# A hybrid encoder layer on one core: other order of PSUM banks in the out projection's second half, later sums for the first MLP tiles, other order of products in the last MLP tile

## The chip, the core and the metric

The kernel runs on one core of a Trainium2 chip. The metric is the device time of one execution in microseconds (us). Five engines share the work, each with an instruction stream of its own: PE (TensorE, matrix products), DVE (VectorE), ACT (ScalarE), POOL (GpSimd) and SP (SyncE, which here only issues DMAs). A semaphore ties an instruction to whatever it has to wait for. The results of PE stand in PSUM banks until DVE or ACT reads them.

## The reference

One encoder layer on 1024 tokens of width 1024, all in fp32: a norm, one projection, two kinds of attention side by side, an out projection with a residual, a gated MLP of inner width 2816 with a short convolution over the tokens, and a last norm.

```python
hn = rmsnorm(h, norm_mix[l])
proj = jnp.einsum('bsd,de->bse', hn, w_in[l])
...
o_a = window_gqa_sink(qa, ka, va, sink[l])
o_b = neighbourhood_attention(...)
mix = jnp.concatenate([rmsnorm(o_a, norm_a[l]), rmsnorm(o_b, norm_b[l])], axis=-1)
h = h + jnp.einsum('bse,ed->bsd', mix, w_out[l])
hn = rmsnorm(h, norm_ffn[l])
# conv_gated_mlp:
g = jnp.einsum('bsd,df->bsf', hn, w_gate)
u = jnp.einsum('bsd,df->bsf', hn, w_up)
g = conv over the tokens, width 3, one filter per channel, + conv_b
h = h + jnp.einsum('bsf,fd->bsd', jax.nn.silu(g) * u, w_down)
return rmsnorm(h, norm_final)
```

## The kernel before, in words

**Layout.** Everything is kept transposed: 128 channels on the partitions, the 1024 tokens along the free axis, in two halves of 512. A PSUM bank holds one 128x512 result. There are four names (tags) of banks with two banks each: `pj`, `o`, `s` and `pt`. Who asks for a bank of a name gets the older of the two, and has to wait until its last reader is done.

**Precision.** Each fp32 factor is split in a high and a low part (`whi`, `wlo` for weights; `hg`, `xd` for operands): ACT makes the high part by a copy (L786), DVE the low part by a subtraction (L787). A block of 128x128 weights is then three matmuls on 512 columns: whi by the high operand (L797, in the attention part L113), whi by the low operand (L798, L114), wlo by the high operand (L799, L115). A product of four blocks is 12 matmuls. So the first matmul of a product waits for `whi`, and the third for `wlo`.

**Who sets the order.** PE runs in the order in which the program is written (`manual_schedule` for PE). On DVE, ACT, POOL and SP a scheduler orders the instructions, starting from the program's order. Buffers come from pools with a fixed number for each tag: 16 `xg`, 14 `op` and 8 `mix` (128x1024 each), 6 `tt` (128x512), 3 `raw` weights, 9 `wh` and 9 `wl`. A load or a result waits until the buffer that it takes over has been read for the last time.

**Out projection.** Its first half (`OutA`, result added by DVE in L490) runs as filler in the attention. The second half is the loop from L857 over the token halves h (2) and the output tiles d (8): a product of 4 blocks in a bank whose name changes from product to product (L861), then `settle_out` (L816) for it: DVE adds the bank to h1, ACT writes h1 to DRAM and squares it for the next norm.

**MLP, gate and up.** Gate and up, the two halves of the tokens and the two halves of the inner dimension make a 2x2 by 2x2 block product, which is done with 7 products in place of 8 (Winograd's form). For a tile of 128 of the 2816 channels (there are 22) `Gated` has these seven methods, each a product of 12 matmuls and what reads its bank:
- `p1`: x = w11 by B11; ACT copies x to c (L937)
- `p5`: y = s1 by t1; DVE adds to c (L947)
- `p6`: z = s2 by t2; DVE makes the second half of gs (L953)
- `p2`: x += w12 by B21; ACT copies x to gs (L942)
- `p3`: y += s4 by B22; DVE adds to gs (L957)
- `conv`: ACT (L963), DVE twice (L964, L965), ACT with Silu (L966), on 128x1024
- `p7`: z += s3 by t3; DVE adds to c (L970)
- `p4`: z += w22 by t4; DVE adds to c (L975) and multiplies c by the conv's result (L976); `keep` writes c to DRAM (a DMA issued by ACT)

A product that adds to a bank has to wait until the reader of the bank's first state is done: `p2` for L937, `p7` for L953, `p3` for L947, `p4` for L970.

The weights of a tile come from `Weights`, one step each: load (SP), w11, w12, s1 (a DVE sum, L903), s2 (L907), s4 (L911), s3 (L916), 22, all but the load with a split. The steps for the next tile are called between the products of the present one (`more`, `w_next.step`).

The tiles are taken in pairs, k and k+11. The first four tiles (`units`, `HEAD` = 4) go product by product through all four; then the main loop (L1126) takes the tiles 4 to 21 one by one, in the order p1, p5, p4 of the tile before (`pend`), p6, p2, p3, conv, p7. In the last tile (21) there are no weights left to prepare, and the order is p1, p2, p5, p4 of tile 20, p6, p7, p3; the first loads for the down projection stand between (`prepare`: weights, `x_load`: operands, both issued by SP).

**Sums.** The down projection has the same seven products, with w_down and the MLP's result as factors. What it needs of a pair are differences: `sums` (L994 ff) makes t2, t3 and t4 for a pair from the two c tiles (three DVE subtractions of 128x512, L835), and `keep` writes them to DRAM (two DMA issues on ACT, one for t2 and t3, one for t4). In the head it is called after `p4` of units 1 and 3; in the main loop after `p4` of a pair's second tile, that is, in every other tile from tile 6 on.

**MLP, down.** 84 groups (7 products, 4 column blocks, 3 parts of K) of up to 12 matmuls. Weights are loaded 6 groups ahead and split 4 groups ahead (`prepare(i + 6, i + 4)`); operands are loaded (`x_load`, L1104, into an `xg` or an `op` buffer) and split (`x_split`, L1110 on ACT, L1111 on DVE) during the product before. `leave` and `finish` add, norm and write the output.

Of the kernel before, what the change touches and what calls it, by code (L numbers as in the profile page):

```python
# [20 lines left out]
KT = D // 128  # L21
# [30 lines left out]
def hybrid_layer(tc, xT, w_in, w_out, w_gate, w_up, w_down, small, sink, rpb, consts, rope, out):  # L52
    nc = tc.nc
    with ExitStack() as ctx:
# [19 lines left out]
        def bank(name, tag):  # L74
            return psum.tile([128, HALF], F32, name=name, tag=tag)
# [41 lines left out]
        def product(ps, ws, xs, h):  # L117

            for i, (w, x) in enumerate(zip(ws, xs, strict=True)):
                block(ps, w, x, h, i == 0, i == len(ws) - 1)  # L120
                yield
# [23 lines left out]
        def inverse_narrow(sqs, dim, tag):  # L145

            ps = bank("ss", tag)
            for c in range(4):
                for i, sq in enumerate(sqs):
                    nc.tensor.matmul(ps[:, c:c + 1], sq[:, c * 128:(c + 1) * 128], ones[:, 0:1], start=c == 0 and i == 0,  # L150
                                     stop=i == len(sqs) - 1, skip_group_check=True)
            v = cpool.tile([128, 4], F32, name="v4", tag="v4", bufs=4)
            nc.scalar.activation(v, ps[:, 0:4], AF.Sqrt, bias=eps, scale=float(D) / dim)
            nc.vector.reciprocal(v, v)
            return v

        def widen(v, tag):

            wide = bank("sw", tag)
            for c in range(4):  # L160
                nc.tensor.matmul(wide[:, c * 128:(c + 1) * 128], v[:, c:c + 1].to_broadcast([128, 128]), ident, start=True, stop=True)
            return wide
# [496 lines left out]
        units = []  # L659
# [38 lines left out]
        sums = {}  # L698
# [10 lines left out]
        pend = None  # L709
        run_q(q_until(1, 4 + AHEAD))  # L710
        fill(FILL1)
        for u in range(len(flat)):
# [14 lines left out]
            for what, e in events:  # L727
                if what == "t":
                    nxt = e()
                elif what == "v":  # L730
                    if pend is not None:
                        pend()
                    pend = nxt
# [14 lines left out]
        def load_wo(d, pools):  # L748
            raw = pools.tile([128, 4, 128], F32, name="raw", tag="raw", bufs=2 if pools is wpool else 3, padded_shape=[128, 4 if pools is wpool else 8, 128])
            nc.sync.dma_start(raw, w_out[d, :, 4:8, :])  # L750
            t = big("wo", "op", F32R)[:, :].rearrange("p (s j c) -> p s j c", s=2, c=128)
            nc.scalar.activation(t[:, 0], raw, AF.Copy)
            nc.vector.tensor_tensor(t[:, 1], raw, f32(t[:, 0]), op=ALU.subtract)
            return [(t[:, 0, j, :], t[:, 1, j, :]) for j in range(4)]
# [46 lines left out]
        def operand(src, tag):  # L801

            t = big("hg", tag, F32R)
            nc.scalar.activation(t[:, 0:HALF], src, AF.Copy)
            nc.vector.tensor_tensor(t[:, HALF:S], src, f32(t[:, 0:HALF]), op=ALU.subtract)
            return t[:, 0:HALF], t[:, HALF:S]
# [7 lines left out]
        def settle_out():  # L814
            d, h, ps = late.pop(0)
            nc.vector.tensor_tensor(at(d, h), ps, at(d, h), op=ALU.add)  # L816
            nc.scalar.dma_start(spilled[d][:, tsl(h)], at(d, h))
            s2 = half("s2")
            nc.scalar.activation(s2, at(d, h), AF.Square)
            if total[h] is not None:  # L820
                nc.vector.tensor_tensor(s2, s2, total[h], op=ALU.add)
            total[h] = s2

        def normed(h, wide, ds):
            for d in ds:
                nc.vector.scalar_tensor_tensor(at(d, h), at(d, h), col(C_NFFN + d), wide, op0=ALU.mult, op1=ALU.mult)

        def pure(f):
            raw = load_raw(w_gate[f], KT)
            W[f, "11"], W[f, "12"] = split_w(raw[:, 0:4], 4), split_w(raw[:, 4:8], 4)  # L830
# [8 lines left out]
        def head_weights(i, name):  # L839
            f, t = FO[i], wsum[i]  # L840
            if name == "s1":
                u = load_raw(w_up[f], KT)
                nc.vector.tensor_tensor(t, u[:, 0:4], u[:, 4:8], op=ALU.add)
            elif name == "s2":
                g = load_raw(w_gate[f, :, 0:4], 4)
                sub(t, t, g)
            elif name == "s4":
                g = load_raw(w_gate[f, :, 4:8], 4)
                sub(t, g, t)
            elif name == "s3":  # L850
                g, u = load_raw(w_gate[f, :, 0:4], 4), load_raw(w_up[f, :, 0:4], 4)
                sub(t, g, u)
            else:
                t = load_raw(w_up[f, :, 4:8], 4)
            W[f, name] = split_w(t, 4)

        for h in range(2):  # L857
            for d in range(KT):
                if h == 0 and d + 2 < KT:
                    wo.append(load_wo(d + 2, fpool))  # L860
                ps = bank("pj", ("pj", "o", "s")[(h * KT + d) % 3])  # L861
                for _ in product(ps, wo[d], mg[4:8], h):
                    pass
                late.append((d, h, ps))
                if h == 1 and d == 1:
                    v = inverse_narrow([total[0]], D, "pt")
                settle_out()
                if h == 0 and d in (3, 4):
                    pure((0, FT // 2)[d - 3])
                if h == 0 and d >= 5 or h == 1 and d == 0:  # L870
                    head_weights((d - 5) % KT, "s1")
                if h == 1 and d == 2:
                    wide = widen(v, "pt")
                    normed(0, wide, K1)
                    B[1, 1] = [operand(at(k, 0), "xg") for k in K1]
                if h == 1 and d == 4:
                    normed(0, wide, K2)
                    B[2, 1] = [operand(at(k, 0), "xg") for k in K2]
# [116 lines left out]
        def sums(unit):  # L995
            k = unit.f % FH
            a, b = first_of.pop(k), unit.c
            t = big("t23", "mix")
            sub(t[:, 0:HALF], b[:, HALF:S], a[:, HALF:S])
            sub(t[:, HALF:S], t[:, 0:HALF], a[:, 0:HALF])  # L1000
            keep(t, ("t2", k), ("t3", k))
            t4 = half("t4")
            sub(t4, b[:, 0:HALF], t[:, 0:HALF])
            keep(t4, ("t4", k))

        units = [Gated(f, ("o", "o", "pj", "pj")[i], ("s", "s", "pt", "pt")[i]) for i, f in enumerate(FO[:HEAD])]
# [44 lines left out]
        w_next = Weights(FO[HEAD])  # L1051
        for i, u in enumerate(units):
            u.p4()
            if i % 2:
                sums(u)
            w_next.step(3)
            if i < 2:
                units[i + 2].conv()
# [42 lines left out]
        def x_load(p, k):  # L1101
            t = big("xd", "xg" if counts[0] % (2 * FH) < 16 else "op", F32R)
            counts[0] += 1
            nc.sync.dma_start(f32(t[:, HALF:S]), X[PRODUCTS[p][1], k])  # L1104
            xraw[p, k] = t
# [10 lines left out]
        def prepare(loads, weights):  # L1116

            while loaded[0] < min(loads, len(order)):
                down_raw(*order[loaded[0]])
                loaded[0] += 1  # L1120
            while made[0] < min(weights, len(order)):
                down_weights(*order[made[0]])
                made[0] += 1

        pend = None
        for i, f in enumerate(FO[HEAD:]):  # L1126
            u = Gated(f)
            w_next.step(9)
            last_one = i + 1 == FT - HEAD
            w_next = None if last_one else Weights(FO[HEAD + i + 1])  # L1130
            more = lambda n=1: w_next.step(n) if w_next else None
            more()
            u.p1()
            if last_one:
                u.p2()
                prepare(2, 0)
            more()
            u.p5()
            if pend:
                pend.p4()  # L1140
                if pend.f >= FH:
                    sums(pend)
            more()
            u.p6()
            if last_one:
                for k in range(6):
                    x_load(0, k)
            more()
            if not last_one:
                u.p2()  # L1150
            more()
            if last_one:
                u.p7()
            u.p3()
            u.conv()
            if last_one:
                prepare(3, 1)
            more()
            if not last_one:
                u.p7()  # L1160
            else:
                for k in range(4):
                    x_split(0, k)
                prepare(4, 2)
                for k in range(6, FH):
                    x_load(0, k)
            more()
            pend = u
# [58 lines left out]
        for i, (p, j, c) in enumerate(order):  # L1227
# [6 lines left out]
            ps = banks[p, j]  # L1234
# [118 lines left out]
```

## Time and profile before

The span goes from the first to the last instruction of the profiled execution.

| what | value |
|---|---|
| time, median of 3 runs | 1135.11 us (1134.78 to 1135.58) |
| time of the profiled execution | 1135.27 us |
| its span | 1133.5 us |
| mean granted TensorE clock | 0.983 |
| busy: PE, PE's weight loads, DVE | 1087.3, 904.3, 853.2 us |
| busy: ACT, POOL | 549.9, 105.9 us |

The stages behind the attention, from the trace (busy time of PE, DVE and ACT in each, and the share of time in which the DMA engines moved data):

| stage | from, to (us) | length | PE | DVE | ACT | DMA |
|---|---|---|---|---|---|---|
| out projection, second half | 426.9 to 472.3 | 45.4 | 45.4 | 38.2 | 22.0 | 62% |
| first four MLP tiles | 472.3 to 545.0 | 72.7 | 72.5 | 66.2 | 34.1 | 28% |
| p4 of the head's last, tiles 4 to 20 | 545.0 to 880.5 | 335.5 | 330.5 | 270.0 | 131.2 | 30% |
| last tile, 21 | 880.5 to 906.5 | 26.0 | 22.4 | 21.0 | 15.7 | 73% |
| down projection and end | 906.5 to 1133.5 | 227.0 | 215.1 | 158.2 | 97.5 | 67% |

How to read what follows. A list of waits gives, for each group of instructions, the engine, the operation with its line, then `<-` and what released it, then the sum of the waits in us, their number and the longest. A table of stretches gives, for each, the length, then the busy time (and the number of instructions) of PE, PE's weight loads, DVE, ACT and POOL, then the granted clock of PE (1.00 is full), the busy share of the DMA engines and GB/s. A timeline has the start in us, the duration, the engine, the line, the operation, its output and inputs with their shapes.

### The profile page before, as it was taken

What the parts mean: (1) busy time and instruction counts of PE and PEld (TensorE: products, weight loads), DVE (VectorE), ACT (ScalarE), POOL (GpSimd) and SP (SyncE); (2) the same over time, 40 slices, a digit from 0 to 9 for tenths busy, and PEclk for the clock granted to TensorE, in tenths of its full rate; (3) what the DMA queues carried; (4) which work ended last, traced back from release to release, by engine and by line L of the source; (5) the groups of instructions that cost most, each with busy time, mean ns of one, the idle gap of its engine ahead of it and who ended that gap; (6) DMA issues with size and microseconds to landing.
All of it is one profiled execution on the core that took longest, in us unless ns stands there. A gap on an engine that the chain in (4) does not pass through costs nothing.

```text
span 1133.5 us, 14918 instructions
## 1 busy us (share of the span) xinstructions
PE 1087.3 (96%) x5124; PEld 904.3 (80%) x5124; DVE 853.2 (75%) x1549; ACT 549.9 (49%) x1033; POOL 105.9 (9%) x186
## 2 busy tenths in 40 slices
PE   8969999999999989999899999999999899999995
PEld 6857888888878878888688888888888688888884
DVE  5556888766689667899988778877877868886843
ACT  6335777656667534444443344334343645543531
POOL 0302333232223100000000000000000000000001
PEclk8989999999999999999899999999999999999997
DMA  7252120333215217303432223222322698865723
GB/s 262 61 126 79 52 57 29 80 93 88 74 36 150 94 47 256 134 29 109 181 128 103 102 93 121 103 102 93 121 103 93 222 322 280 280 226 169 258 83 148
DMA packets 67708, 147.03 MB, mean 130 GB/s; under 512 B 8112, under 2 KB 16816, under 8 KB 67632
## 3 DMA queue, kind: packets, MB, share of 16 engines
q1 hardware_dynamic: 57552, 121.04, 33.4%
q10 hardware_dynamic: 10080, 25.04, 5.9%
q8 instruction: 40, 0.66, 0.2%
q14 instruction: 36, 0.29, 0.1%
HBM read 103.58 MB, written 28.57 MB: 117 GB/s over the span
## 4 chain that ended last, share of the span: by engine, by line
PE 87%; DVE 6%; DMA 2%; ACT 2%; issue 1%; SPq 0%; POOLq 0%; ACTq 0%; DVEq 0%
PE pj L113 7%; PE pj L114 7%; PE pj L115 7%; PE dn L797 6%; PE dn L799 6%; PE dn L798 6%; PE z L797 4%; PE z L798 4%; PE z L799 4%; PE s L273 3%; PE x L797 3%; PE x L798 3%; PE x L799 3%; PE y L799 3%; PE y L798 3%; PE y L797 3%
## 5 line engine op out<-in xcount | busy, mean ns | idle before, releaser
L786 ACT ACTIVATE whi<-ws 128x512 fp32r<-128x512 f32 (+1 forms) x100 | 60.1, 623 | 126.2 <-DVE ws L903 86.0
L797 PE MATMUL dn<-xd,whi 128*128 128x512 f32 x308 | 120.0, 390 | 0.0
L799 PE MATMUL dn<-xd,wlo 128*128 128x512 f32 x308 | 119.8, 389 | 0.0
L798 PE MATMUL dn<-xd,whi 128*128 128x512 f32 x308 | 119.8, 389 | 0.0
L797 PE MATMUL z<-hg,whi 128*128 128x512 f32 x264 | 103.2, 391 | 2.2 <-DVE gs L953 2.2
L113 PE MATMUL pj<-xgh,whi 128*128 128x512 f32 x248 | 103.7, 418 | 0.0
L799 PE MATMUL z<-hg,wlo 128*128 128x512 f32 x264 | 103.2, 391 | 0.2 <-DVE wlo L787 0.2
L798 PE MATMUL z<-hg,whi 128*128 128x512 f32 x264 | 103.0, 390 | 0.0
L299 ACT ACTIVATE p<-p,nm 128x385 f32<-128x385 f32 (+3 forms) x128 | 75.1, 587 | 55.5 <-DVE nm L295 51.5
L115 PE MATMUL pj<-xgh,wlo 128*128 128x512 f32 x248 | 97.8, 394 | 0.0
L114 PE MATMUL pj<-xgl,whi 128*128 128x512 f32 x248 | 97.5, 393 | 0.0
L303 POOL TENSOR_SCALAR p<-p,sm 128x384 f32<-128x384 f32 (+1 forms) x128 | 73.2, 584 | 237.1 <-DVE sm L301 217.9
L787 DVE TENSOR_TENSOR wlo<-raw,whi 128x512 fp32r<-128x512 f32 (+1 forms) x102 | 66.7, 672 | 24.2 <-ACT whi L786 24.2
L786 ACT ACTIVATE whi<-raw 128x512 fp32r<-128x512 f32 (+1 forms) x102 | 61.0, 612 | 45.3 <-DMA raw<-in_w_down_dram 11.0
L787 DVE TENSOR_TENSOR wlo<-ws,whi 128x512 fp32r<-128x512 f32 (+1 forms) x100 | 67.0, 683 | 20.6 <-ACT whi L786 20.4
L309 DVE TENSOR_TENSOR pl<-pt,ph 128x384 fp32r<-128x384 f32 (+2 forms) x108 | 63.2, 588 | 23.2 <-ACT ph L308 22.1
L308 ACT ACTIVATE ph<-pt 128x384 fp32r<-128x384 f32 (+2 forms) x108 | 55.2, 513 | 38.4 <-PE pt L408 30.9
L1209 POOL TENSOR_TENSOR y<-y,wide 128x512 f32<-128x512 f32 x4 | 5.1, 1280 | 734.1 <-ACT y L1208 734.1
L1110 ACT ACTIVATE xd<-xd 128x512 fp32r<-128x512 f32 x77 | 47.5, 627 | 53.5 <-DMA xd<-x 51.7
L797 PE MATMUL y<-hg,whi 128*128 128x512 f32 x176 | 69.3, 394 | 2.9 <-ACT whi L786 2.9
L799 PE MATMUL y<-hg,wlo 128*128 128x512 f32 x176 | 69.6, 395 | 2.2 <-DVE wlo L787 2.2
L797 PE MATMUL x<-hg,whi 128*128 128x512 f32 x176 | 68.8, 391 | 1.4 <-ACT c L937 1.4
(199 smaller groups left out, 2660.7 us busy)
## 6 DMA issues: line engine op xcount, KB each, us to landing
xd<-x SPq DMA_DIRECT2D x77, 256.0 KB, 4.9
raw<-in_w_down_dram SPq DMA_DIRECT2D x72, 256.0 KB, 3.5
raw<-in_w_gate_dram SPq DMA_DIRECT2D x22, 512.0 KB, 3.5
raw<-in_w_up_dram SPq DMA_DIRECT2D x22, 512.0 KB, 3.8
x<-c ACTq DMA_DIRECT2D x22, 512.0 KB, 2.8
raw<-in_w_in_dram SPq DMA_DIRECT2D x32, 256.0 KB, 3.2
raw<-in_w_down_dram SPq DMA_DIRECT2D x36, 192.0 KB, 3.8
x<-t ACTq DMA_DIRECT2D x11, 512.0 KB, 5.8
```

What stands on the lines that cost most here:

```text
L113: nc.tensor.matmul(ps, w[0], x[0][:, tsl(h)], start=first, stop=False)
L114: nc.tensor.matmul(ps, w[0], x[1][:, tsl(h)], start=False, stop=False)
L115: nc.tensor.matmul(ps, w[1], x[0][:, tsl(h)], start=False, stop=last)
L299: nc.scalar.activation(p[:, j, 0:e], p[:, j, 0:e], AF.Exp, bias=nm, scale=-1.0, accum_out=sm[:, j:j + 1])
L303: nc.gpsimd.tensor_scalar(p[:, i, 0:m], p[:, i, 0:m], sm[:, i:i + 1], 1.0, op0=ALU.mult, op1=ALU.mult)
L308: nc.scalar.activation(ph[:, 0:n], ps[:, 0:n], AF.Copy)
L309: nc.vector.tensor_tensor(pl[:, 0:n], ps[:, 0:n], f32(ph[:, 0:n]), op=ALU.subtract)
L786: nc.scalar.activation(hi, src, AF.Copy)
L787: nc.vector.tensor_tensor(lo, src, f32(hi[:, :, :]), op=ALU.subtract)
L797: nc.tensor.matmul(ps, w[0], x[0], start=first and i == 0, stop=False, skip_group_check=True)
L798: nc.tensor.matmul(ps, w[0], x[1], start=False, stop=False, skip_group_check=True)
L799: nc.tensor.matmul(ps, w[1], x[0], start=False, stop=last and i == len(ws) - 1, skip_group_check=True)
```

## The change

Three edits, all in the program's order. None adds or removes a computation.

1. The banks of the out projection's second half go in the order `o`, `s`, `pj` in place of `pj`, `o`, `s`.
2. `sums` of the head's units 1 and 3 is no longer called behind their `p4`, but in the main loop behind `p6` of tile 4 (for unit 1) and of tile 5 (for unit 3).
3. In the last tile p2 goes where the other tiles have it (behind p6), so that the order is p1, p5, p4 of tile 20, p6, p2, p7, p3. The first two loads of down weights stand behind p5 and p4 in place of p2, and of the six operand loads, four stay behind p6 and two go behind p2.

```diff
@@ -858,7 +858,7 @@
-                ps = bank("pj", ("pj", "o", "s")[(h * KT + d) % 3])
+                ps = bank("pj", ("o", "s", "pj")[(h * KT + d) % 3])
@@ -1051,8 +1051,6 @@
         for i, u in enumerate(units):
             u.p4()
-            if i % 2:
-                sums(u)
             w_next.step(3)
@@ -1122,7 +1120,7 @@
-        pend = None
+        pend, owed = None, [units[1], units[3]]
         for i, f in enumerate(FO[HEAD:]):
@@ -1131,25 +1129,27 @@
             u.p1()
-            if last_one:
-                u.p2()
-                prepare(2, 0)
             more()
             u.p5()
             if pend:
                 pend.p4()
                 if pend.f >= FH:
                     sums(pend)
+            if last_one:
+                prepare(2, 0)
             more()
             u.p6()
+            if owed:
+                sums(owed.pop(0))
             if last_one:
-                for k in range(6):
+                for k in range(4):
                     x_load(0, k)
             more()
-            if not last_one:
-                u.p2()
+            u.p2()
             more()
             if last_one:
+                for k in range(4, 6):
+                    x_load(0, k)
                 u.p7()
             u.p3()
             u.conv()
```

Line numbers in what follows are those of the kernel before; from the second edit on the changed kernel's are two lower in the functions of the down projection.

## The prediction

> **What bounds the kernel now.** First the page: its chain of work that ended last is PE for 87%, and PE is busy 96% of the span. Time can come only from stretches in which PE stands or runs slowly, so the second view is the list of what PE waited for, over the whole span. All of it is 30 us; five of its lines lie behind the attention:
> ```profile
> PE 87%; DVE 6%; DMA 2%; ACT 2%; issue 1%; SPq 0%; POOLq 0%; ACTq 0%; DVEq 0%
> ```
> ```profile
> PE pj L113 <- DVE h L490: 3.5, 2, 3.2
> PE y L797 <- ACT whi L786: 2.9, 1, 2.9
> PE y L799 <- DVE wlo L787: 2.2, 1, 2.2
> PE z L797 <- DVE gs L953: 2.2, 1, 2.2
> PE x L797 <- ACT c L937: 1.4, 1, 1.4
> ```
> The two y waits stand at 553.9 to 559.9, in the first tile of the main loop (tile 4): its weights s1 are not split. The last two are in the last tile (tile 21), at 883.2 and 895.9. The third view is a table of stretches (PE, PEld, DVE, ACT, POOL busy, then the granted clock):
> ```profile
> 418.90:422.30 3.40, 1.93 (x9) 1.26 (x7) 3.40 (x7) 1.90 (x3) 0.00 (x0) 1.00 0.00 0
> 422.30:425.70 3.40, 1.66 (x7) 1.39 (x8) 2.89 (x5) 0.63 (x1) 0.00 (x0) 1.00 0.00 0
> 555.45:558.85 3.40, 0.73 (x2) 0.30 (x2) 3.40 (x5) 0.63 (x1) 0.00 (x0) 1.00 0.58 231
> 558.86:565.68 6.82, 5.80 (x14) 4.56 (x15) 6.73 (x11) 3.17 (x5) 0.00 (x0) 0.50 0.39 148
> ```
> After the stretch with PE busy for 0.73 of 3.40 us the clock is halved for 6.8 us; after stretches with half of it busy it is not. And DVE is full. Its timeline there, with the part that goes away in the middle:
> ```profile
> 550.88 1.22 DVE L976 TENSOR_TENSOR c<-c,cv 128x1024 f32<-128x1024 f32 x1
> 552.01 0.68 DVE L975 TENSOR_TENSOR c<-z,c 128x512 f32<-128x512 f32 x1
> 552.62 0.68 DVE L835 TENSOR_TENSOR t<-c 128x512 f32<-128x512 f32 x1
> 553.22 1.22 DVE L976 TENSOR_TENSOR c<-c,cv 128x1024 f32<-128x1024 f32 x1
> 554.35 0.68 DVE L835 TENSOR_TENSOR t<-t,c 128x512 f32<-128x512 f32 x1
> 554.95 0.68 DVE L835 TENSOR_TENSOR t<-c,t 128x512 f32<-128x512 f32 x1
> 555.55 0.68 DVE L903 TENSOR_TENSOR ws<-raw 128x512 f32<-128x512 f32 x1
> ...
> 559.15 0.68 DVE L787 TENSOR_TENSOR wlo<-ws,whi 128x512 fp32r<-128x512 f32 x1
> ```
> The three L835 rows from c to t are sums(units[1]); L903 makes s1, L787 its low half. Starts also give the spacing that I use: 0.60 us for a 128x512 on DVE, 1.13 for L976, 1.19 for L964 or L965; a result stands 0.69 after its start. PE at full clock starts a matmul each 0.2266 us (472.32 to 480.25, 35 steps), so a product of 12 takes 2.72.
>
> **Part 1, banks.** The 3.2 us at 424.05 are the last product of the half before (it reads whi, not wo). The first wo product starts at 426.92 without a wait. With the new order its bank was left by the attention at 402.3; the pj bank comes third, at 432.4, and its last reader L490 ends at 427.8. In the MLP the second x product (475.04) has its bank free from 473.9, and in the new order one product sooner. The instruction order on DVE and ACT does not change in this stage. **0**; were a cover gone, one eviction, 0.7 us.
>
> **Part 2, sums.** What tile 4 loses now: its y should start at 553.94; its 18th matmul after that starts at 566.10, not at 553.94 + 17 x 0.2266 = 557.79. That is **8.3 us**: 3.0 and 2.4 in the waits, the rest at half clock; from there PE runs without a wait up to 883.
>
> I go through the new order by hand, with the rows' durations. Up to L976 at 550.88 nothing moves. Then DVE: L903 at 552.01, L975 552.62, L916 553.22, L976 553.82, low half of s1 at 554.95, done 555.64. ACT: its L966 ends 552.11, one DMA issue, then the high half of s1 at 552.75, done 553.38: in time. PE starts y at 553.94, its third matmul, due 554.40, at 555.69: **1.29 us**. Next DVE: L964 555.55, L907 556.74, L965 557.34, low half of s2 at 558.53, done 559.22; ACT makes the high half 557.47 to 558.10. PE's z is due 558.07: 0.1, and its third matmul 0.55 more. s4, s3 and 22 are split by 563.4, 564.0 and 564.6; PE wants the first at 564.8, the others later: no wait. Tile 5: its sums, three rows from 566.26 with L957 between them (waits for PE, 567.45), L903 at 569.25, L964, L970, L965, low half of s1 at 572.84, done 573.53; PE is due there at 572.98: 0.6. In tile 5 sums(units[3]) comes after L953 at 582.8, and tile 6's s1 is done 588.4 for a PE that wants it at 592.7: 4 us of slack, so it is over. With 0.1 for restarts after each stop the new loss is 1.3 + 0.65 + 0.6 + 0.4 = 3.0. **Gain 5.3 us.** The moved sums, 3 x 0.60 each, go to tiles 4 and 5, which have none of their own; DVE is busy 30.7 of 40 us in a steady stretch (640 to 680), 4.4 us free per tile of 19.0. Their three DMA issues each (0.33 us) go to ACT with them, and ACT is busy 14.7 of 40. SP's and POOL's orders stay as they are up to the last tile. The c tiles are held longer; the new waits that this puts on tiles 5 to 7 are on writes issued some 20 us before. Bounds: gain 2.6 (below) to 8.3.
>
> The new stops are 1.3 us at most, so no stretch of 3.4 us falls under half busy, and by the rows above the clock stays. [...]
>
> **Part 3, last tile.** Now: x, x2, y, 22 of tile 20, z, z2 (p7), y2 (p3), 22. The waits are 884.83 - 883.23 = 1.60 (x2 adds to the bank that L937 still has to copy, and L937 stands behind L966 on ACT) and 898.20 - 895.86 = 2.34 (z2 adds to the bank that L953 reads; L953 stands on DVE behind operand splits L1111 and L976). From 880.51 to the first down product, 906.49, it is 25.98; eight products are 21.76. Loss **4.2 us**, 0.3 of it restarts.
>
> New: x 880.51, y 883.23, 22 885.95, z 888.67, x2 891.39, z2 894.11, y2 896.83, 22 899.55, down 902.27. x2 wants L937, done 884.8: 6.6 us of room. z2 wants L953. On DVE behind the split at 884.26 stand 12 rows before it: a weight 884.86, two operands, L947, two operands, a weight 888.46, L975 889.06, operand 4 889.66, L976, operand 5 891.39, L835, then L953 892.59, done 893.28: 0.8 us of room. Operands 4 and 5 now take the buffers of the y product, so SP issues them at 884.1 and 884.8, behind four others and before two weight loads; the landing time of these loads is 3.0 to 5.9 us. At 5.9 operand 4 is 1 us late and z2 waits 0.25. The last 22 wants L970, behind seven more rows: done 898.1 for 899.55; a landing of 5.9 would cost 0.3. L942 moves behind x2, and L963 with it; only the late conv waits for that. **Gain 4.2** (3.0 to 4.2 by these bounds).
>
> **Down products.** PE comes there 9.5 us earlier, DMA is busy 93% (906 to 940). The distance from the end of a weight's low half to the first matmul that reads it is 21 us at the start and 4.9 at the least (1076.8 to 1081.7). The loads and splits wait for buffers that PE frees, so they move along: 0.
>
> **Sum** against the profiled execution, 1135.27 (span 1133.5, the median of the runs is 1135.11): 1135.3 - 5.3 - 4.2 = **1125.8**, 0.84% less.
>
> **Rivals.**
> [...] 0.05.
> B, the last tile's waits return at another product, L953 or L970 behind later loads: up to the old 2.3 again, 1128.1. For it: the room of 0.8. 0.10.
> C, the moved sums meet tiles 5 and 6 with DVE still full: 2 x 1.8, 1129.4. For it: DVE has no gap from 546 to 572. 0.06.
> D, the down products are paced by their loads, which keep their times: only 4.9 us can be kept, 1130.4. For it: DMA at 93%. Against: distances of 12 us in that stretch. 0.06.
> E, all of the 8.3 goes: 1122.8. 0.03.
> F, **slower**: on SP the load of operand 10, which waits for tile 20's c to be written, now stands before three weight loads. That write leaves ACT at about 894 and lands about 3 us later; the first weight behind it is read at 918.6 and needs some 5 us, so from 17 us late on each further one is lost, and from 26 the kernel is slower, 1136 and up. 0.03.
> That the order is not what the text says is excluded by the order on each engine, which I used. For A to D together, no change: 0.04. **Forecast 0.63**, by itself 1124.3 to 1127.3.
>
> 0.2% is 2.3 us, about what a measurement of this kernel tells from no change. Faster (below 1132.8): 0.63 + 0.05 + 0.10 + 0.06 + 0.06 + 0.03 = 0.93; same 0.04; slower 0.03. The range runs from 1123.5 to 1129.8, with A, B and C in it.
>
> **What would show it.** Right: PE's waits for s1 in tile 4 near 1.3 with a clock of 1.00 from 552 to 570; none for L937 and L953 in the last tile; first down product 9.5 us earlier and no PE wait behind it. Wrong: a granted clock of 0.50 there, a wait for wlo in tiles 5 or 6, a PE wait in the down products, or a wait at L113 for another bank.

## The result, and the profile after

The changed kernel takes 1129.11 us (median of 13 runs, 1125.19 to 1135.59), the kernel before 1135.19 beside it (13 runs, 1134.44 to 1140.12). That is 6.1 us less by the medians; the ratio over all runs is 0.9941 (95% interval 0.9928 to 0.9954), which makes 6.7 us. Forecast were 1125.8. The profiled execution took 1127.34 us, its span is 1125.6 against 1133.5.

The page's chain of the changed kernel, and PE's waits between 400 and 1118 us (sum, number, longest):

```profile
PE 86%; DVE 7%; DMA 3%; ACT 2%; issue 2%; SPq 0%; POOLq 0%; ACTq 0%; DVEq 0%
```
```profile
PE pj L113 <- DVE h L490: 3.4, 2, 3.2
...
PE dn L797 <- ACT c L1218: 1.1, 1, 1.1
PE z L799 <- DVE wlo L787: 0.7, 2, 0.4
...
PE y L799 <- DVE wlo L787: 0.5, 2, 0.3
```

Of the two y waits in tile 4 the first (2.9) is gone and the second (2.2) has shrunk to 0.2; the other y wait in the list, 0.3, is in tile 5. Both waits of the last tile (L953, L937) are gone too. There is one new line, `dn L797 <- ACT c L1218`: the second down product waits for ACT to copy the first one's bank.

The table of stretches of 3.41 us, counted from the times at which the granted clock changes (length, PE, PE's loads, DVE, ACT, POOL, then the clock):

```profile
420.32:423.73 3.41, 0.55 (x2) 0.48 (x3) 3.41 (x7) 1.26 (x2) 0.00 (x0) 1.00 0.00 0
423.74:427.14 3.40, 3.40 (x9) 2.65 (x8) 0.58 (x1) 0.00 (x0) 0.00 (x0) 0.50 0.00 0
```
```profile
553.45:556.85 3.40, 3.23 (x14) 2.36 (x13) 3.40 (x5) 1.42 (x2) 0.00 (x0) 1.00 0.15 59
556.86:560.26 3.40, 3.00 (x13) 1.92 (x12) 3.40 (x6) 1.78 (x3) 0.00 (x0) 1.00 0.00 0
```

In tile 4 PE is now busy for 3.0 of 3.4 us or more, and the clock stays at 1.00. At 423.7, where the kernel before kept the full clock, there is a new half one, behind the 3.2 us wait that no edit touches.

Where the 7.9 us of span went, by the start of the same instructions in both traces:

| stretch | before | after | difference |
|---|---|---|---|
| start to the first MLP product | 472.32 | 473.03 | +0.71 |
| to p1 of the last tile | 408.19 | 401.75 | -6.44 |
| last tile, to the first down product | 25.98 | 22.04 | -3.94 |
| first down product (132 matmuls) | 29.92 | 31.21 | +1.29 |
| the other six down products, last matmul | 181.18 | 181.31 | +0.13 |
| from there to the end | 15.89 | 16.21 | +0.32 |

The new wait, in ACT's timeline of the changed kernel (start, duration; in brackets the idle time before a row and what ended it):

```profile
917.98 0.63 ACT L1108 ACTIVATE xd<-xd 128x512 fp32r<-128x512 f32 x1 [1.42 <-DMA xd<-x]
918.52 0.51 ACT L786 ACTIVATE whi<-raw 128x384 fp32r<-128x384 f32 x1
920.74 0.63 ACT L1108 ACTIVATE xd<-xd 128x512 fp32r<-128x512 f32 x1 [1.71 <-DMA xd<-x]
921.27 0.62 ACT L786 ACTIVATE whi<-raw 128x512 fp32r<-128x512 f32 x1
924.57 0.63 ACT L1108 ACTIVATE xd<-xd 128x512 fp32r<-128x512 f32 x1 [2.68 <-DMA xd<-x]
925.10 0.62 ACT L786 ACTIVATE whi<-raw 128x512 fp32r<-128x512 f32 x1
926.86 0.63 ACT L1108 ACTIVATE xd<-xd 128x512 fp32r<-128x512 f32 x1 [1.14 <-DMA xd<-x]
927.40 0.58 ACT L1218 ACTIVATE c<-dn 128x512 f32<-128x512 f32 x1
```

The first bank is complete near 921, and the copy of 0.58 us is made at 927.40, after four operand splits that each waited for a load. PE wants the bank at 926.74 and gets it at 928.03. These splits (L1108) are of the operands t1 of the **third** product, which starts at 958. In the kernel before the same four stand ahead of the same copy. The last of them, the copy, and the matmul of PE that wants it:

```profile
933.37 0.63 ACT L1110 ACTIVATE xd<-xd 128x512 fp32r<-128x512 f32 x1 [3.44 <-DMA xd<-x]
933.91 1.03 ACT L786 ACTIVATE whi<-raw 128x512 fp32r<-128x512 f32 x2
934.85 0.58 ACT L1218 ACTIVATE c<-dn 128x512 f32<-128x512 f32 x1
936.41 0.39 PE L797 MATMUL dn<-xd,whi 128*128 128x512 f32 x1
```

The copy ends at 935.43 there and PE wants it at 936.41, so 0.98 us of room were left, and no list of waits shows it.

### The profile page after: what moved, and what is told of

The parts are those of the page before. It is cut to its first block, busy times and chain, and to the rows that moved or that the text cites. A ratio compares the mean times of both kernels' runs of the same rounds, so it can differ in the third digit from the quotient of the medians.

```text
span 1125.6 us, 14912 instructions
## 1 busy us (share of the span) xinstructions
PE 1086.2 (96%) x5124; PEld 903.0 (80%) x5124; DVE 852.4 (76%) x1549; ACT 548.3 (49%) x1033; POOL 105.7 (9%) x186
## 4 chain that ended last, share of the span: by engine, by line
PE 86%; DVE 7%; DMA 3%; ACT 2%; issue 2%; SPq 0%; POOLq 0%; ACTq 0%; DVEq 0%
PE pj L113 7%; PE pj L114 7%; PE pj L115 7%; PE dn L797 6%; PE dn L799 6%; PE dn L798 6%; PE z L799 5%; PE z L797 5%; PE z L798 5%; PE x L797 3%; PE x L799 3%; PE x L798 3%; PE s L273 3%; PE y L799 3%; PE y L797 3%; PE y L798 3%
## 5 line engine op out<-in xcount | busy, mean ns | idle before, releaser
L797 PE MATMUL dn<-xd,whi 128*128 128x512 f32 x308 | 120.2, 390 | 1.1 <-ACT c L1218 1.1
L113 PE MATMUL pj<-xgh,whi 128*128 128x512 f32 x248 | 103.4, 417 | 0.0
L797 PE MATMUL z<-hg,whi 128*128 128x512 f32 x264 | 102.9, 390 | 0.0
L1108 ACT ACTIVATE xd<-xd 128x512 fp32r<-128x512 f32 x77 | 47.3, 627 | 58.0 <-DMA xd<-x 56.5
L797 PE MATMUL x<-hg,whi 128*128 128x512 f32 x176 | 68.7, 390 | 0.0
L799 PE MATMUL x<-hg,wlo 128*128 128x512 f32 x176 | 68.5, 389 | 0.0
```

The costliest lines, as they stand in the source:

```text
L113: nc.tensor.matmul(ps, w[0], x[0][:, tsl(h)], start=first, stop=False)
L797: nc.tensor.matmul(ps, w[0], x[0], start=first and i == 0, stop=False, skip_group_check=True)
L799: nc.tensor.matmul(ps, w[1], x[0], start=False, stop=last and i == len(ws) - 1, skip_group_check=True)
```

## The experiments

All were timed in five rounds beside the kernel before, whose medians were 1135.3 to 1136.3 in these comparisons. Ratios are to it, over all runs; what a version gains in us is worked out from its ratio.

**One edit each.** First the banks alone (`("o", "s", "pj")` in L861):

> Only the order of banks (edit 1). Theory: no bank is waited for behind the 3.2 us at 424, so 0 within 1 us, and the list of PE's waits behind 402 us as before. Rival (the banks matter, because DVE's and ACT's readers come in another order): over 1 us either way, with another wait at L113 or in the first x products.

1136.43 us, ratio 0.9994 (0.9982 to 1.0006). No new wait at L113; the first MLP product starts at 471.67. The banks are worth nothing, as both the expectation and the prediction had it. This profile of the old order of the last tile shows a wait of 0.6 for L1218: the room of 0.98 us is not even always there.

Then the sums alone:

```diff
             u.p4()
-            if i % 2:
-                sums(u)
...
-        pend = None
+        pend, owed = None, [units[1], units[3]]
...
             u.p6()
+            if owed:
+                sums(owed.pop(0))
```

> Only the sums of units 1 and 3 moved (edit 2). Theory: tile 4 loses 1 to 3 us in place of 8.3, no half clock at 555 to 570, so 5.5 to 7 us less than before (ratio 0.994 to 0.995), as steady from run to run as before, because nothing is near its limit behind tile 5. Rival (the spread of the changed kernel, 1125 to 1136, comes from DVE being full in tiles 4 to 6): the times of this kernel spread as far.

1131.05 us (1128.9 to 1133.2), ratio 0.9942 (0.9921 to 0.9963), 6.6 us less. From the first MLP product to the last tile it is 401.75 us, to 0.1 us the same as in all seven other profiles with moved sums. With the old place it is 408.19, 406.66, 406.69, 406.64 and 406.10 in five. So no spread from profile to profile is left in this stretch. In this profile the last tile, in its old order, lost more than in the first; the wait for L953 and the stretches at it:

```profile
PE z L797 <- DVE gs L953: 3.2, 1, 3.2
```
```profile
891.91:895.32 3.41, 0.69 (x3) 0.60 (x4) 3.41 (x6) 0.96 (x2) 0.00 (x0) 1.00 0.01 4
895.33:898.73 3.40, 3.40 (x10) 2.62 (x9) 1.05 (x2) 0.00 (x0) 0.00 (x0) 0.50 0.78 256
```

Behind the wait of 3.2 us, which lies in one stretch of 3.41, PE runs 3.40 us at a clock of 0.50. By the author's estimate, half of that, this costs 1.7 us more.

Then the last tile alone (edit 3):

> Only the last tile's order (edit 3). Theory: its two waits (1.6 and 2.3) go, the first down product starts 3.8 us earlier, but the first down products now meet operand loads that have not landed, so that 1 to 4 us come back as PE waits behind 920 us; on the mean 1 to 3 us less than before, with a spread of several us from run to run. Rival (the loads move along with PE, as the prediction had it): 3.8 to 4.2 us less, with a spread like that of the kernel before.

1134.49 us (1129.64 to 1138.63), ratio 0.9982 (0.9963 to 1.0001), 2.0 us less. The last tile takes 22.20 us, as expected; the first down product takes 32.46 in place of 29.92, and PE's list has the reason:

```profile
PE dn L797 <- ACT c L1218: 2.4, 1, 2.4
```

So the loads did not simply move along with PE. The expectation, that 1 to 4 us come back behind 920 us, is met, but PE waits for a copy and not for an operand. The spread is not explained by it: these times lie 9.0 us apart, those of the kernel before beside them 6.9.

**The changed kernel again.**

> The changed kernel as it is, for a second profile on the same chip. Theory (the spread comes from the down projection's loads): stage by stage the same up to 897 within 1 us apart from where the clock's windows fall, and the difference from the first profile in waits of PE between 920 and 1080. Rival (the spread comes from the clock alone): the same waits, other stretches at half clock.

1129.27 us, ratio 0.993 (0.9912 to 0.9948). Up to the last tile the second profile differs from the first only by the front and the clock. In the last tile it waits 0.2 for L953 and 0.5 for L970, so that tile takes 23.10; for L1218 it waits 2.1 (1.1 in the first profile). The expectation is met in part only: of the 3.4 us between the two spans 0.9 are in the first down product, 1.1 in the last tile, 0.8 in the front and 0.6 at the end.

**What the copy waits for.** First the residual loads, which SP issues among the operand loads, while the DMA is 92% busy (896.82 to 928.03 in the changed kernel):

```diff
-for place, what, up, h in ((4, residual, 0, 0), (12, residual, 1, 1), (16, residual, 0, 1), (20, add_first, 1, 1),
+for place, what, up, h in ((10, residual, 0, 0), (18, residual, 1, 1), (22, residual, 0, 1), (24, add_first, 1, 1),
```

> The changed kernel, with the twelve residual loads of 256 KB (h, L1178) that now run between 902 and 935 us asked for six groups of the down projection later; nothing else in the program moves. Theory (the operand loads of the second down product are late because they share a DMA that is 90% busy with these loads, and ACT's copy of the first bank, L1218, stands behind their splits): the wait of 1.1 to 2.4 us for L1218 goes, and the time is 1 to 2.5 us under the changed kernel's, about 0.991 of before. Rival (the operand loads are held up by their place in SP's queue behind weight loads that wait for a free buffer, whatever the DMA moves): the wait stays within 0.5 us of 1 to 2.4, the time equals the changed kernel's 0.993 to 0.994.

1129.93 us, ratio 0.9944 (0.9927 to 0.996); the wait is 3.4. That the wait would go is wrong, and 3.4 is above the rival's range too. But the edit was no clean test: the scheduler set the other instructions anew, and seven of the residual loads are still issued up to 919 us (in the changed kernel nine up to 924, where PE is 3.1 us later). What it did show is ACT's queue. Five splits of the third product's operands stood ahead of the copy, not four, and the last of them waited longest:

```profile
926.01 0.63 ACT L1108 ACTIVATE xd<-xd 128x512 fp32r<-128x512 f32 x1 [5.90 <-DMA xd<-x]
926.54 0.58 ACT L1218 ACTIVATE c<-dn 128x512 f32<-128x512 f32 x1
```

Then the copies on DVE:

```diff
-                nc.scalar.activation(c_at(j), ps, AF.Copy)
+                nc.vector.tensor_copy(c_at(j), ps)
```

> The changed kernel, with the four copies of the first down product (L1218) on DVE in place of ACT, where they stand one operand split earlier. Theory (the loads are late themselves): the wait for L1218 shrinks or goes, but PE then waits at nearly the same time for the operand that the same loads bring, so under 1 us is won. Rival (the copy's place in ACT's queue is the whole cause): 1 to 2.4 us are won and no PE wait follows.

1128.99 us, ratio 0.9932 (0.9914 to 0.995), and a wait of 2.0 for the copy, now on DVE. Neither expectation was met: DVE makes the low halves of the same operands, so the copy stands behind the same loads there, and it tells nothing apart.

**The order taken away.** Here the third product's operands may be loaded only when the copies are made. One column of the operand's buffer, written by POOL from the copy, makes the load wait; the load overwrites it:

```diff
             counts[0] += 1
+            if p == 2 and k < 8:
+                nc.gpsimd.tensor_copy(t[:, HALF:HALF + 1], c_at(k // 2)[:, 0:1])
             nc.sync.dma_start(f32(t[:, HALF:S]), X[PRODUCTS[p][1], k])
```

In the changed kernel:

> The changed kernel, in which the first eight operands of the third down product (t1) may be loaded only when the first product's copies (L1218) are made: POOL, else idle here, writes one element of each operand buffer from the copy ahead of the load. So no split of these operands, which PE needs only 30 us later, stands ahead of the copies on ACT any more. Theory (the wait of 1.1 to 3.4 us at the second down product comes from ACT's order alone: copies behind splits of operands that are not yet needed and whose loads are late): the wait goes, the copy follows its product within 2 us, and the time is 1.5 to 3.5 us under the changed kernel's, ratio 0.990 to 0.992. Rival (the loads themselves pace the down products): a wait of like size for another operand or a weight's low half, no gain; or the third product waits for its late operands.

1125.16 us (1123.92 to 1129.3), ratio 0.9914 (0.9888 to 0.9939). With edit 3 alone:

> Edit 3 alone (the last tile's order), with the same dependence of the third product's operands on the copies. Theory: now the last tile's gain stays, 3.5 to 4 us and some half clock with it, ratio 0.9955 to 0.997, where edit 3 alone gave 0.998. Rival (the down products are paced by loads): 0.998 again.

1131.34 us (1129.63 to 1132.18), ratio 0.996 (0.9944 to 0.9977), 4.5 us less where edit 3 alone gave 2.0 (the two intervals overlap a little). In the kernel before:

> The kernel before, with the same dependence. There the copy has about 1 us of room, so theory: no change, 0.999 to 1.001. Rival (the dependence helps by itself, whatever the last tile does): over 1.5 us less.

1135.88 us, ratio 1.0001 (0.9987 to 1.0016). The dependence is worth nothing by itself; it gives back what the last tile's order had won. ACT in the first of the three (L1220 is the copy there):

```profile
922.63 0.63 ACT L786 ACTIVATE whi<-raw 128x512 fp32r<-128x512 f32 x1 [0.71 <-DMA raw<-in_w_down_dram]
924.37 0.53 ACT L786 ACTIVATE whi<-raw 128x384 fp32r<-128x384 f32 x1 [1.11 <-DMA raw<-in_w_down_dram]
924.80 0.58 ACT L1220 ACTIVATE c<-dn 128x512 f32<-128x512 f32 x1
```

No split of the third product's operands stands ahead of the copy; weight splits still do, and it is made some 2 us before PE asks. The first down product in this kernel and in the changed one (length, PE busy):

```profile
897.43:927.35 29.92, 29.92 (x134) 24.77 (x133) 19.90 (x30) 14.26 (x24) 1.31 (x2) 1.00 0.91 305
```
```profile
896.82:928.03 31.21, 30.08 (x133) 24.59 (x131) 20.41 (x31) 15.22 (x27) 0.00 (x0) 1.00 0.92 309
```

DMA is as busy in both (0.91 and 0.92). The loads are late in the changed kernel, but PE does not need yet what they bring; it waited for them because of the order on ACT. Both kernels once more on one chip:

> The changed kernel once more, on one chip with the version whose third product's operands wait for the copies. Theory: 1128 to 1130 us, a wait for L1218 of 1 to 3.5 us in the profile. Rival (the two kernels do not differ but in the luck of where the clock's windows fall): medians within 1 us of each other.

> The version in which the third product's operands wait for the copies, a second time. Theory: 1.5 to 4 us under the changed kernel on the same chip, no PE wait in the down products. Rival (luck of the clock's windows): within 1 us of the changed kernel.

1129.03 us (ratio 0.9943, 0.9925 to 0.9961; a wait of 2.7 for L1218) and 1126.88 us (0.9917, 0.9896 to 0.9939; no wait in the down products). The wait is gone in both profiles of the second kernel and there in all three of the first; the sign of the difference in time came out twice, its size (2.2 us here, about 4 the first time, when the changed kernel did not run beside it) is less sure, as the intervals overlap.

**The clock.** The kernel before, with PE kept busy in the waits of tile 4 (L879 is the line that does it; it is broken into several here):

```diff
+mm = lambda ps, w, x, first, last: nc.tensor.matmul(ps, w, x, start=first, stop=last, skip_group_check=True)
+idle = lambda ps, w, x, n: [mm(ps, w, x, True, True) for _ in range(n)]
+def filled(y, ws, xs, ps, w):
+    idle(ps, w, xs[0][0], 8)
+    mm(y, ws[0][0], xs[0][0], True, False); mm(y, ws[0][0], xs[0][1], False, False)
+    idle(ps, w, xs[0][0], 8)
+    mm(y, ws[0][1], xs[0][0], False, False); group(y, ws[1:], xs[1:], False, True)
...
-group(self.y, W[self.f, "s1"], B["t1"], True, True)
+group(self.y, W[self.f, "s1"], B["t1"], True, True) if self.f != FO[HEAD] else filled(self.y, W[self.f, "s1"], B["t1"], bank("spare", "pt"), W[self.f, "12"][0][0])
```

> The kernel before, with 16 matmuls into a spare bank, that nobody reads, in PE's two waits for s1 in tile 4 (8 ahead of y's first matmul, 8 ahead of its third). The waits for the split of s1 stay, PE is busy in them. Theory (the clock is halved after a window of 3.4 us in which PE is little busy): the clock stays at 1.00 between 552 and 570, y's third matmul starts as late as before, and 2.7 to 3.4 us are won of the 8.3 (ratio 0.997 to 0.998). Rival (the half clock has another cause than PE's low busy share there): half clock as before, no gain or a loss up to 1 us.

1133.83 us, ratio 0.998 (0.9967 to 0.9992), 2.3 us less, somewhat under the 2.7 to 3.4 us expected. The stretches of tile 4:

```profile
554.56:557.96 3.40, 3.32 (x16) 2.43 (x15) 3.40 (x5) 1.28 (x3) 0.00 (x0) 1.00 0.51 204
557.97:561.37 3.40, 3.03 (x13) 2.18 (x14) 3.40 (x6) 1.06 (x1) 0.00 (x0) 1.00 0.61 243
```

y's third matmul still starts 5.2 us after x's last one (6.2 before), but the clock stays at 1.00. With the sums in their old place and PE idle in the waits it falls to 0.50 in this tile: in the kernel before (558.86 to 565.68, behind a stretch with 0.73 us of PE work), with the banks alone (from 556.06, behind 1.49) and with the last tile alone (557.66 to 561.06, behind 1.04). So the half clock of tile 4 comes from PE's idle time there.

## Why the prediction was right or wrong

**Banks, 0:** right, 0.9994.

**Sums, gain 5.3:** the mechanism is right, and the size is within 1.1 us: 6.44 in the profiled pair. DVE's order is the one worked out by hand, row by row (L903 551.72, L975 552.32, L916 552.92, L976 553.52, low half of s1 at 554.66). Only the stop for s1 is 0.33 and not 1.29 us. In the profile of before DVE had waited 0.87 us at 546.08 for ACT's high half of a weight whose load was late (ACT stood 3.63 us for it, up to 545.41); that profile was unlucky there by 1.5 to 2.1 us, as the other four with the old place of the sums show (406.1 to 406.7 in place of 408.2). Against those the gain is 4.4 to 4.9. So the 8.3 us lost before were 1.5 to 2.1 more than in those profiles, and the new loss of 3.0 was too high as well (1.9: 401.75 against 408.19 - 8.31). That the two errors cancel is luck. The stops at z and in tile 5 make PE 0.7 and 0.45 us late, near the 0.65 and 0.6 forecast, and no other wait follows in tiles 5 to 7: rivals C and E are out.

**Half clock, rival A (it stays in tile 4):** out. The prediction had it right that in tile 4 the clock follows the busy share. In the traces of the kernel before and of the changed kernel the times at which the granted clock changes lie whole multiples of 3.413 us apart (in the changed kernel 427.14 - 423.73 = 3.41, and 1113.22 - 427.14 = 201 x 3.413). The two traces have these times at different places (408.67 and 412.08 before, 406.66 and 410.08 after). Cut there, they have 399 stretches at full clock from 415 to 1100 us. Two are followed by half clock, with 0.73 and 0.55 us of PE work; the least in the others is 1.69 (before, from 422.32). Stretches of other profiles lie between: behind 0.69 (the sums alone, and the later residuals), 1.04 (the last tile alone) and 1.49 (the banks alone) the clock is halved, behind 1.57 (the last tile alone, from 929.71) and 1.59 (the changed kernel again, from 927.19) it is not.

The range from 415 to 1100 us matters, for the busy share does not decide everywhere. In both traces the clock is also halved between 406 and 413 us behind a stretch in which PE is busy throughout (3.40 us in the one, 3.41 in the other). In the kernel before (length, PE busy, then as above):

```profile
405.26:408.66 3.40, 3.40 (x27) 3.25 (x28) 0.06 (x1) 1.08 (x3) 0.00 (x0) 1.00 0.00 1
408.67:412.08 3.41, 3.41 (x9) 2.65 (x9) 0.84 (x3) 0.00 (x0) 0.00 (x0) 0.50 0.43 154
```

Of the 27 matmuls there 23 are sums with one column (L150), where those behind 415 us have 512 almost without exception. Why the clock falls there no run tests. In the last norm it falls after stretches with 2.07 us of PE work (before, 1118.65 to 1122.05) and 1.76 (after, 1109.81 to 1113.21).

**Last tile, gain 4.2 (3.0 to 4.2):** right in the profile, 3.94. In the eight other profiles with this order the tile takes 22.2 to 23.1 us, 0.4 to 1.4 above the 21.76 of its eight products. But the 25.98 before were the least of five profiles with the old order; the others have 26.34, 27.56, 28.65 and 28.66, and with the sums alone the wait for L953, 3.2 there, is followed by a stretch at half clock (895.33 to 898.73), which the prediction's sum left out. By the medians of all profiles, 27.56 and 22.54, the gain is 5.0. The waits left in PE's lists, 0.2 to 0.3 for L953 and 0.3 to 0.6 for L970, are the two that the prediction named, 0.25 and 0.3.

**Down products, 0:** this is the step that failed. It looked at the weights' low halves, whose distance to PE stays 3.5 us at the least (at 1021 us; 4.9 before), and found that "the loads and splits wait for buffers that PE frees, so they move along". ACT's copies L1218 were not looked at. They end a chain that does not move along: SP's loads of the third product's operands stand behind weight loads, and are issued only 3.9 to 5.5 us earlier than before (914.06, 916.43, 920.22, 923.10 for 918.08, 920.35, 925.76, 927.97), while PE reaches its second product 9.7 us earlier. With 0.98 us of room that gives a wait of 1.29 in the profiled run, 2.2 to 3.6 in the five other profiles of this order without the dependence; in that with the later residuals a stretch at half clock follows the wait (0.50 from 927.87 to 931.27, behind 0.69 us of PE work). The prediction had named a PE wait in the down products as a sign that it is wrong. Rival D had the sign and the place (less of the last tile's gain is kept) but named the wrong resource. Rival B is there as 0.1 to 0.8 us in eight of the nine profiles and not as 2.3; of F, late weights behind SP's wait for tile 20's c, no profile shows a trace.

**The sum.** 1125.8 forecast and 1127.34 profiled differ by 1.5: -1.1 (sums), +0.3 (last tile), +1.4 (down products), +0.7 (front and the half clock at 423.7, behind the 3.2 us wait, which leaves 0.55 us of PE work in one stretch here, but 1.93 and 1.66 in two at full clock in the profile of before), +0.3 (end). Of the two gains the profiled pair shows one too large and one too small: by the medians over all profiles they are 4.9 and 5.0, and their sum is near the 9.5 forecast, so what is missing is in the main the wait for L1218. The median of 1129.11 us lies inside the range for all cases (1123.5 to 1129.8) but above the 1124.3 to 1127.3 given for the forecast itself. It is 1.8 above the profiled run, whose waits in the last tile and for L1218 are the smallest of the three profiles of this kernel. What the slowest runs (up to 1135.6) lost was not profiled.

## What to carry to other kernels

When PE is made to arrive earlier, check every instruction that releases it in the stage behind, the copies out of its banks too, and ask of each what stands ahead of it in its engine's queue; a split of an operand that is needed 30 us later can hold up a copy that is needed now. A wait that has 1 us of room is in no list of waits: the room has to be worked out from the two ends. And take a wait's cost from more than one profile where it hangs on a load, and count the half clock with it.

## What the runs showed of the hardware

Between 415 and 1100 us, where PE runs almost only matmuls of 512 columns, the granted clock fell to 0.50 behind stretches of 3.41 us with 0.55 (changed kernel), 0.69 (sums alone, later residuals), 0.73 (before), 1.04 (last tile alone) and 1.49 us (banks alone) of PE work, and did not behind 1.57 (last tile alone) and 1.59 (changed kernel again). At 405.26 to 408.66 of the kernel before, where 23 of 27 matmuls have one column, it fell behind 3.40.

The same wait of 3.2 us at L113 lies in one stretch in the changed kernel (0.55 us of PE work), and 3.40 us at 0.50 follow, with matmuls 0.43 us apart in place of 0.23. In the kernel before it lies in two (1.93 and 1.66), and the clock stays at 1.00. From the matmul behind the wait to the first wo product it is 4.45 us in the first (423.18 to 427.63) and 2.87 in the second (424.05 to 426.92), 1.58 less.

A second half stretch followed in the kernel before, where PE was busy for 2.39 us of the first (558.86 to 562.27). Where PE was busy throughout the half stretch, the full clock came back: before (562.27 to 565.68), changed kernel (423.74 to 427.14), last tile alone (557.66 to 561.06), sums alone (895.33 to 898.73).
